# Loading one operand three tiles ahead instead of four in a batched 64x64 matmul

## The chip, the cores and the metric

The kernel runs on one core of a Trainium2 chip, the other cores idle. In the profiles PE is TensorE (PEld its weight loads), DVE is VectorE, ACT is ScalarE, POOL is GpSimd and SP is SyncE; SP, ACT and POOL also issue the DMA transfers, and a load lands when its bytes are all in place. The metric is the device time of one execution in microseconds (us), as the median of several runs. All comparisons below use runs that were marked fast; a ratio is the mean time of one kernel's fast runs over the mean time of the other kernel's fast runs of the same rounds, so it is not quite the ratio of the two medians that stand beside it.

## The reference

```python
a = np.random.randn(1024, 64, 64).astype(np.float32)
b = np.random.randn(1024, 64, 64).astype(np.float32)
out = np.matmul(a, b).astype(np.float32)
```

Each of the three tensors is 16.78 MB. There is little arithmetic for that many bytes, so the kernel is mostly a matter of moving data.

## The kernel before

The batch is cut into 16 tiles of 64 matrices. Tile `t` of b is 1 MB and lives in one of `B_AHEAD` buffers. a comes in 8 steps of 128 matrices; three quarters of a step are loaded from POOL's queue and cast to bf16 on the way (`a_sb`), the last quarter is loaded raw from SP's queue (`a_raw`). Only the first step is loaded raw as a whole, from SP and ACT. Even tiles of b are issued on SP, odd ones on ACT. Stores are issued on POOL.

```python
    A_AHEAD = 3
    B_AHEAD = 4
    HOLD = 2
    # ...
    b_pool = ctx.enter_context(tc.tile_pool(name="b_pool", bufs=B_AHEAD))
    o_pool = ctx.enter_context(tc.tile_pool(name="o_pool", bufs=8))
    # ...
    def load_b(t):
        b_sb = b_pool.tile([128, 16, 128], fp32, name="b_sb")
        queue = nc.scalar if t % 2 else nc.sync
        queue.dma_start(out=b_sb[:], in_=b_v[t])
        b_tiles[t] = b_sb
    # ...
        for t in range(n_t):
            s, half = t // 2, t % 2
            if t + 1 < n_t:
                spread(t + 1)            # VectorE: a into block-diagonal form
                cast(t + 1)              # VectorE: b to bf16, frees the b buffer
            if t + B_AHEAD < n_t:
                load_b(t + B_AHEAD)      # waits for the cast of tile t
            if half == 0 and 0 < s < n_s - 1 - A_AHEAD:
                load_a(s + 1 + A_AHEAD)
            # ...
            multiply(t)                  # TensorE, then copies out of PSUM on ACT and VectorE
            if t == 0:
                regroup(1)
                load_a(A_AHEAD)
                load_a(A_AHEAD + 1)
            # ... regroup (VectorE), transpose (TensorE, ACT) of later steps of a
            if t >= HOLD - 1:
                store(t - HOLD + 1)      # POOL's queue
```

The last tile but one is stored in two pieces and the last in four; all others in one piece of 1 MB.

Of the kernel before, what the change touches and what calls it, by code (L numbers as in the profile page):

```python
# [13 lines left out]
def kernel(  # L14
# [18 lines left out]

    n_t, n_s = B // 64, B // 128
    A_AHEAD = 3
    B_AHEAD = 4
    N_BD = 2
    HOLD = 2

# [5 lines left out]
    a_pool = ctx.enter_context(tc.tile_pool(name="a_pool", bufs=A_AHEAD))  # L45
    b_pool = ctx.enter_context(tc.tile_pool(name="b_pool", bufs=B_AHEAD))
    work = ctx.enter_context(tc.tile_pool(name="work", bufs=2))
# [16 lines left out]
    def load_a(s):  # L64

        a_sb = a_pool.tile([128, 3, 16, 64], bf16, name="a_sb")
        for h in range(3):
            nc.gpsimd.dma_start(  # L68
                out=a_sb[:, h, :, :].rearrange("p v k -> p (v k)"), in_=a_v[s, h]
            )  # L70
        a_raw = a_pool.tile([128, 16, 64], fp32, name="a_raw")
        nc.sync.dma_start(out=a_raw[:].rearrange("p v k -> p (v k)"), in_=a_v[s, 3])  # L72
        a_tiles[s] = a_sb, a_raw

    def load_first_a():

        raw = [
            o_pool.tile([128, 8, 2, 2, 64], fp32, name="o_sb")[:].rearrange(
                "p gh j wl n -> p (gh j wl n)"
            )  # L80
            for _ in range(2)
        ]
        parts = [raw[h % 2][:, 1024 * (h // 2) : 1024 * (h // 2) + 1024] for h in range(4)]
        for h in range(4):
            (nc.scalar if h % 2 else nc.sync).dma_start(out=parts[h], in_=a_v[0, h])  # L85
        a_tiles[0] = parts
# [7 lines that stand above are left out]
    def regroup(s):  # L94
        a_sb = a_tiles.pop(s)
        a_bf = work.tile([128, 16, 4, 64], bf16, name="a_bf")
        if s == 0:
            for h in range(4):
                copy = nc.scalar.copy if h % 2 else nc.vector.tensor_copy
                copy(a_bf[:, :, h, :], a_sb[h].rearrange("p (v k) -> p v k", v=16))  # L100
        else:
            cast_sb, raw = a_sb
            nc.vector.tensor_copy(  # L103
                a_bf[:, :, 0:3, :], cast_sb[:].rearrange("p h v k -> p v h k")
            )
            nc.vector.tensor_copy(a_bf[:, :, 3, :], raw[:])  # L106
        abf_tiles[s] = a_bf
        at_tiles[s] = work.tile([128, 2, 32, 2, 4, 4], fp32, name="at_sb")

    def transpose(s, j):  # L110
        a_cols = abf_tiles[s][:].rearrange("p v h k -> p v (h k)").bitcast(fp32)
        for wl in range(2):
            at_ps = t_psum.tile([128, 4, 128], fp32, name="at_ps")
            for vo in range(4):
                nc.tensor.transpose(  # L115
                    at_ps[:, vo, :], a_cols[:, 4 * vo + 2 * j + wl, :], identity[:]
                )
            nc.scalar.copy(  # L118
                at_tiles[s][:, j, :, wl, :, :],
                at_ps[:].rearrange("p vo (g mp) -> p g mp vo", mp=4),  # L120
            )

    def spread(t):
        half = slice(16 * (t % 2), 16 * (t % 2) + 16)
        bd = bd_tiles[t % N_BD]
        for h in range(4):
            rows = slice(32 * h, 32 * h + 32)
            nc.vector.tensor_copy(  # L128
                bd[rows, :, :, :, h, :].rearrange("p j g wl mo -> p j (g wl) mo"),
                at_tiles[t // 2][rows, :, half, :, :, :].rearrange(  # L130
                    "p j g wl mp vo -> p j (g wl) (mp vo)"
                ),
            )

    def cast(t):
        b_bf = work.tile([128, 16, 128], bf16, name="b_bf")
        b_sb = b_tiles.pop(t)
        if t < n_t - 1:
            (nc.vector.tensor_copy if t else nc.scalar.copy)(b_bf[:], b_sb[:])  # L139
        else:  # L140
            for gq in range(4):
                rows = slice(4 * gq, 4 * gq + 4)
                if gq % 2:
                    nc.vector.tensor_copy(b_bf[:, rows, :], b_sb[:, rows, :])
                else:
                    nc.scalar.copy(b_bf[:, rows, :], b_sb[:, rows, :])  # L146
        bbf_tiles[t] = b_bf

    def store(t):
        for piece in held.pop(t):  # L150
            piece()
# [53 lines left out]
    with tc.manual_schedule():  # L205
        load_first_a()

        nc.vector.memset(warm[:, 0:1], 0.0)
        nc.scalar.copy(warm[:, 1:2], warm[:, 0:1])  # L209
        load_b(0)  # L210
        load_b(1)
        nc.vector.memset(bd_tiles[0][:], 0.0)  # L212
        make_identity(nc, identity)
        nc.gpsimd.memset(bd_tiles[1][:, 0], 0.0)
        load_a(1)
        load_b(2)
        nc.gpsimd.memset(bd_tiles[1][:, 1], 0.0)  # L217
        load_a(2)
        regroup(0)
        transpose(0, 0)  # L220
        transpose(0, 1)
        load_b(3)
        spread(0)
        cast(0)
        for t in range(n_t):
            s, half = t // 2, t % 2
            if t + 1 < n_t:
                spread(t + 1)
                cast(t + 1)
            if t + B_AHEAD < n_t:  # L230
                load_b(t + B_AHEAD)
            if half == 0 and 0 < s < n_s - 1 - A_AHEAD:
                load_a(s + 1 + A_AHEAD)
            if half == 0 and 0 < s < n_s - 1:
                transpose(s + 1, 1)
            multiply(t)
# [4 lines that stand above are left out]
                transpose(1, 0)  # L241
                transpose(1, 1)
            elif t == 1:
                regroup(2)
            elif half == 0 and s + 2 < n_s:
                regroup(s + 2)
            if half == 1 and s + 2 < n_s:
                transpose(s + 2, 0)
            if t >= HOLD - 1:
                store(t - HOLD + 1)  # L250
        for t in range(n_t - HOLD + 1, n_t):
            store(t)
# [30 lines left out]
```

## Time and profile before

| what | value | where it is read |
|---|---|---|
| median time | 135.42 us (135.24 to 135.50) | 3 runs |
| span of the profiled run | 133.8 us | head of the page |
| read and written | 33.55 MB and 16.78 MB | the HBM line |
| VectorE busy, ACT busy | 71%, 66% | part 1 |
| last b tile issued, landed | 94.05 us, 110.45 us | timeline of ACT, 16.4 us to landing |
| last product copied out of PSUM | 121.37 us | timeline of ACT, 118.34 + 3.03 |
| last store issued | about 122.4 us | timeline of POOL |

Busy shares of 71% and 66% suggest that no engine is the limit, and over the whole span none is. The row of the DMA engines tells more, because it is full from the second slice to the last but one. The prediction shows these lines. A detail for reading them is that a load with a cast counts its written bytes, half of what it reads, so slices with many of them show about 310 GB/s although the engines are no less busy.

### The profile page before, as it was taken

Reading aid. Unit: us, or ns where it says so; the run is one execution under the profiler, and the core shown is the slowest. Engines: PE = TensorE matmul, PEld = TensorE weight load, DVE = VectorE, ACT = ScalarE, POOL = GpSimd, SP = SyncE. Lnnn points to the kernel's source line nnn. Section 1 sums busy time; section 2 is a strip of 40 time slices with the busy share of each in tenths; the row PEclk is TensorE's granted clock in tenths of the full one; section 3 lists DMA queues with packets and bytes.
Section 4 is the critical chain, followed back from the end, with each engine's and each line's share of the span. In section 5 each row is a group of like instructions: output and inputs, shape, how many; then the busy total and the mean of one; then the engine's idle time right before and its main releaser. Section 6 shows DMA issues by size and latency. Waiting matters only on the chain.

```text
span 133.8 us, 2832 instructions
## 1 busy us (share of the span) xinstructions
PE 65.7 (49%) x1152; PEld 62.7 (47%) x1152; DVE 94.6 (71%) x120; ACT 87.7 (66%) x161; POOL 38.5 (29%) x49
## 2 busy tenths in 40 slices
PE   0007307970077463749919744991876376640000
PEld 0007207970077353649909744991866266630000
DVE  5930499108997059999999999899959989992000
ACT  3225424998038996758998985899793987992000
POOL 8991000420091080334124042003301220637000
PEclk9999999999559999555996896589677775797555
DMA  3999999999999999999999999999999999999991
GB/s 75 376 331 311 306 315 311 307 301 309 306 307 382 366 312 309 388 397 397 317 304 352 399 392 377 314 307 364 398 385 391 392 401 398 404 388 353 338 334 42
DMA packets 17485, 45.01 MB, mean 336 GB/s; under 512 B 1088, under 2 KB 1088, under 8 KB 17472
## 3 DMA queue, kind: packets, MB, share of 16 engines
q0 software_dynamic: 7440, 22.28, 54.8%
q1 hardware_dynamic: 5520, 13.11, 27.0%
q10 hardware_dynamic: 4512, 9.44, 18.6%
q8 instruction: 9, 0.15, 0.4%
q14 instruction: 4, 0.03, 0.1%
HBM read 33.55 MB, written 16.78 MB: 376 GB/s over the span
## 4 chain that ended last, share of the span: by engine, by line
DMA 35%; SPq 27%; DVE 15%; issue 6%; ACT 3%; POOL 3%; PE 3%; POOLq 1%; DVEq 0%; ACTq 0%
SPq L72 22%; DMA a_raw<-in_a_dram 18%; DMA b_sb<-in_b_dram 17%; DVE at_bd L128 8%; DVE b_bf L139 5%; SPq L91 3%; POOL out_dram L161 3%; PE o_ps L184 3%; ACT o_sb L172 2%; DVE o_sb L172 1%; SPq L85 1%; ACT b_bf L146 1%; DVE a_bf L106 1%; DVE a_bf L103 1%; POOLq L278 1%
## 5 line engine op out<-in xcount | busy, mean ns | idle before, releaser
L172 ACT COPY o_sb<-o_ps 64x512 f32<-64x512 f32 x106 | 61.6, 581 | 14.3 <-PE o_ps L184 13.0
L184 PEld LDWEIGHTS <-at_bd 128*128 128x128 bf16 x1024 | 41.6, 111 | 34.9 <-DVE b_bf L139 22.4
L184 PE MATMUL o_ps<-b_bf,at_bd 128*128 128x64 bf16 x960 | 41.9, 215 | 31.1 <-DVE b_bf L139 20.9
L128 DVE COPY at_bd<-at_sb 32x1024 f32<-32x1024 f32 x64 | 46.0, 719 | 13.4 <-ACT at_sb L118 11.6
L161 POOL DMA_DIRECT2D out_dram<-o_sb x20 | 20.6, 1031 | 58.1 <-ACT o_sb L172 21.4
L115 PE MATMUL at_ps<-identity,a_bf 128*128 128x128 f32 x128 | 23.4, 360 | 20.6 <-ACT a_bf L100 11.0
L115 PEld LDWEIGHTS at_ps<-identity,a_bf 128*128 128x128 f32 x128 | 21.6, 196 | 20.8 <-issue 19.3
L118 ACT COPY at_sb<-at_ps 128x512 f32<-128x512 f32 x32 | 16.9, 596 | 8.2 <-PE at_ps L115 8.0
L68 POOL DMA_DIRECT2D a_sb<-in_a_dram x21 | 13.9, 673 | 25.9 <-DVE a_bf L103 19.9
L139 DVE CAST b_bf<-b_sb 128x2048 bf16<-128x2048 f32 x14 | 17.4, 1245 | 2.9 <-DMA b_sb<-in_b_dram 2.6
L172 DVE COPY o_sb<-o_ps 64x512 f32<-64x512 f32 x14 | 9.7, 690 | 0.6 <-ACT o_sb L172 0.3
L106 DVE CAST a_bf<-a_raw 128x1024 bf16<-128x1024 f32 x7 | 5.5, 792 | 5.7 <-DMA a_raw<-in_a_dram 5.7
L103 DVE COPY a_bf<-a_sb 128x3072 bf16<-128x3072 bf16 x7 | 7.0, 1006 | 0.0
L100 ACT CAST a_bf<-o_sb 128x1024 bf16<-128x1024 f32 x2 | 2.1, 1044 | 5.0 <-DMA o_sb<-in_a_dram 5.0
L139 ACT CAST b_bf<-b_sb 128x2048 bf16<-128x2048 f32 x1 | 1.9, 1898 | 3.8 <-DMA b_sb<-in_b_dram 3.8
L100 DVE CAST a_bf<-o_sb 128x1024 bf16<-128x1024 f32 x2 | 2.8, 1380 | 1.9 <-DMA o_sb<-in_a_dram 1.9
L212 DVE MEMSET at_bd<- 128x4096 f32 x1 | 3.5, 3472 | 0.8 <-issue 0.8
L172 DVE COPY o_sb<-at_ps 64x256 f32<-64x256 f32 x8 | 3.4, 422 | 0.3 <-PE at_ps L184 0.2
L172 ACT COPY o_sb<-at_ps 64x256 f32<-64x256 f32 x8 | 2.9, 367 | 0.1
L209 ACT ACT_TABLE_LOAD x1 | 1.3, 1283 | 2.3 <-issue 2.3
L184 PE MATMUL at_ps<-b_bf,at_bd 128*128 128x64 bf16 x64 | 2.0, 193 | 1.2 <-DVE at_bd L128 1.2
L217 POOL MEMSET at_bd<- 128x2048 f32 x1 | 1.8, 1849 | 0.0
(12 smaller groups left out, 5.5 us busy)
## 6 DMA issues: line engine op xcount, KB each, us to landing
out_dram<-o_sb POOLq DMA_DIRECT2D x14, 1024.0 KB, 23.6
a_sb<-in_a_dram POOLq DMA_DIRECT2D x21, 256.0 KB, 17.4
a_raw<-in_a_dram SPq DMA_DIRECT2D x7, 512.0 KB, 24.2
o_sb<-in_a_dram ACTq DMA_DIRECT2D x2, 512.0 KB, 7.0
o_sb<-in_a_dram SPq DMA_DIRECT2D x2, 512.0 KB, 5.9
out_dram<-o_sb POOLq DMA_DIRECT2D x2, 512.0 KB, 11.4
out_dram<-o_sb POOLq DMA_DIRECT2D x4, 256.0 KB, 10.1
b_sb<-in_b_dram SPq DMA_DIRECT2D x8, 0.5 KB, 22.2
```

Source lines behind the costliest of these rows:

```text
L68: nc.gpsimd.dma_start(out=a_sb[:, h, :, :].rearrange("p v k -> p (v k)"), in_=a_v[s, h])
L72: nc.sync.dma_start(out=a_raw[:].rearrange("p v k -> p (v k)"), in_=a_v[s, 3])
L100: copy(a_bf[:, :, h, :], a_sb[h].rearrange("p (v k) -> p v k", v=16))
L103: nc.vector.tensor_copy(a_bf[:, :, 0:3, :], cast_sb[:].rearrange("p h v k -> p v h k"))
L106: nc.vector.tensor_copy(a_bf[:, :, 3, :], raw[:])
L115: nc.tensor.transpose(at_ps[:, vo, :], a_cols[:, 4 * vo + 2 * j + wl, :], identity[:])
L118: nc.scalar.copy(at_tiles[s][:, j, :, wl, :, :], at_ps[:].rearrange("p vo (g mp) -> p g mp vo", mp=4),)
L128: nc.vector.tensor_copy(bd[rows, :, :, :, h, :].rearrange("p j g wl mo -> p j (g wl) mo"), at_tiles[t // 2][rows, :, half, :, :, :].rearrange(
L139: (nc.vector.tensor_copy if t else nc.scalar.copy)(b_bf[:], b_sb[:])
L161: nc.gpsimd.dma_start(out=o_v[t, :, lo : lo + n, :], in_=o_sb[:, lo : lo + n].rearrange("p gh j wl n -> p (gh j wl n)"),)
L172: copies[2 * par + wl](dst, src)
L184: nc.tensor.matmul(o_ps[:, gl, g % 2, j, :], at_bd[:, j, g, :, u], b_bf[:, g, 64 * u : 64 * u + 64], start=(u == 0), stop=(u == 1),)
```

## The change

The intent is to need one b buffer less (8 KB of each partition), on the guess that three tiles ahead are enough.

```diff
-    B_AHEAD = 4
+    B_AHEAD = 3
@@
         transpose(0, 0)
         transpose(0, 1)
-        load_b(3)
         spread(0)
         cast(0)
```

## The prediction

> **What bounds the kernel now.** I read the page's slices first, to see whether anything is full all the time.
>
> ```profile
> DVE  5930499108997059999999999899959989992000
> ACT  3225424998038996758998985899793987992000
> DMA  3999999999999999999999999999999999999991
> GB/s 75 376 331 311 306 315 311 307 301 309 306 307 382 366 312 309 388 397 397 317 304 352 399 392 377 314 307 364 398 385 391 392 401 398 404 388 353 338 334 42
> HBM read 33.55 MB, written 16.78 MB: 376 GB/s over the span
> ```
>
> The row to look at is DMA: after the first of the 40 slices (3.3 us each) it never drops below 9 until the last one. The slices with 301 to 317 GB/s are not slack: there the queue from POOL loads a as fp32 and writes it as bf16, and the rate counts the written bytes. The kernel must move 33.55 + 16.78 = 50.33 MB; from about 2.5 us to 131 us that is 50.33 MB / 128.5 us = 392 GB/s. The window table gives the same rate where nothing is cast, and shows the end:
>
> ```profile
> 100.00:110.50 10.50, 5.83 (x128) 5.46 (x128) 9.87 (x13) 7.69 (x14) 2.26 (x2) 0.75 1.03 395
> 110.50:120.00 9.50, 5.66 (x128) 5.38 (x128) 8.76 (x15) 8.59 (x18) 3.03 (x3) 0.74 1.02 397
> 120.00:123.10 3.10, 0.00 (x0) 0.00 (x0) 1.06 (x3) 1.34 (x4) 2.85 (x4) 0.86 1.02 358
> 123.10:126.00 2.90, 0.00 (x0) 0.00 (x0) 0.00 (x0) 0.00 (x0) 0.00 (x0) 0.50 1.02 346
> 126.00:129.00 3.00, 0.00 (x0) 0.00 (x0) 0.00 (x0) 0.00 (x0) 0.00 (x0) 0.50 1.00 341
> 129.00:131.00 2.00, 0.00 (x0) 0.00 (x0) 0.00 (x0) 0.00 (x0) 0.00 (x0) 0.50 0.75 275
> 131.00:132.00 1.00, 0.00 (x0) 0.00 (x0) 0.00 (x0) 0.00 (x0) 0.00 (x0) 0.50 0.10 41
> ```
>
> The last two columns are DMA share and GB/s. All engines are done at about 123 us; for 8 us more the DMA engines only drain stores. So the end is set by bytes, not by the last product. In the middle VectorE is nearly full too (9.70 of 10 us in 50 to 60, 9.67 and 9.74 in the next two), which paces a b tile at about 5.9 us (the casts start at 51.70, 57.51, 63.36, 68.91, 75.01 us). Because VectorE runs ahead of the stores, a backlog of stores builds up, and that backlog is the 8 us at the end.
>
> Next I read who waits for a load:
>
> ```profile
> DVE a_bf L106 <- DMA a_raw<-in_a_dram: 5.7, 1, 5.7
> DVE b_bf L139 <- DMA b_sb<-in_b_dram: 2.6, 4, 1.5
> SPq L91 <- DVE b_bf L139: 2.2, 3, 1.3
> ```
>
> Waits for b cost VectorE 2.6 us in all, in four pieces. So four buffers are just enough: some b tiles arrive within a fraction of a microsecond of their use.
>
> **What the Trainium skill says.** "DMA: Bandwidth & Descriptors", section "Issuing engines are not separate DMA queues", says that copies issued from SP, ACT and POOL run on the same 16 engines and interleave. The trace agrees: b alone on ACT's queue takes 15.6 to 17.4 us from issue to landing for 1 MB, far longer than 1 MB at 392 GB/s (2.7 us). The same page, "Queues, rings and completion order", says each engine takes turns between queue rows packet by packet. I use that for the share that a queue gets: when one queue has nothing, the others get its turns. "HBM Reference", "Specifications (TRN2)", puts a core streaming alone at about 425 GB/s, bounded by its 16 engines; this trace sustains 392 to 397, so the page's figure leaves at most some 8% that this kernel does not reach before or after.
>
> **The change part by part.** No instruction of compute is added or removed, and no byte: 16 loads of b remain, of 1 MB each. One b buffer disappears, so the load of tile t+4 waits for the cast of t+1 instead of the cast of t, and it stands one turn of the loop later in its queue. The order of the built program shows three shifts.
>
> First, b tile 3 leaves the prologue. It was issued on ACT at 14.77 us; now it stands after the cast of tile 0 there (19.07 + 1.90 us), so at about 21 us, 6 us later. It landed at 14.77 + 16.8 = 31.6 us and was cast at 40.16, so 8.6 us of slack cover that. By 14.77 us, without b tile 3, these had been asked for: a's first 2.1 MB, three tiles of b (3.1 MB), two raw quarters of a (1 MB), nine cast quarters (4.7 MB read): 11 MB, or 28 us of work at 392 GB/s. DMA does not run dry.
>
> Second, on SP the third and fourth raw quarters of a now stand ahead of b tile 4.
>
> ```profile
> 23.19 0.71 SPq L91 DMA_DIRECT2D b_sb<-in_b_dram  x1
> 23.95 13.28 SPq L72 DMA_DIRECT2D a_raw<-in_a_dram  x2
> 48.22 0.69 DVE L106 CAST a_bf<-a_raw 128x1024 bf16<-128x1024 f32 x1 [5.71 <-DMA a_raw<-in_a_dram]
> ```
>
> Before, the raw quarters queued behind 1 MB of b, and VectorE stood 5.71 us for the first. With b behind them I expect the quarter some 8 us earlier (1 MB at the 115 GB/s that SP's queue got here, 1.5 MB between b landings 13 us apart) and most of that wait gone. B tile 4 then lands about 5 us later, at 51 instead of 46.1, against a cast at 51.70. So some 3 to 5 us come back there, part of them lost again to b.
>
> Third, the steady part. Issues on SP and their landings:
>
> ```profile
> 53.02 0.71 SPq L91 DMA_DIRECT2D b_sb<-in_b_dram  x1
> 64.74 0.71 SPq L91 DMA_DIRECT2D b_sb<-in_b_dram  x1
> 70.22 0.70 ACTq L91 DMA_DIRECT2D b_sb<-in_b_dram  x1
> 82.13 0.70 ACTq L91 DMA_DIRECT2D b_sb<-in_b_dram  x1
> 94.05 0.69 ACTq L91 DMA_DIRECT2D b_sb<-in_b_dram  x1
> ```
>
> The two on SP (tiles 8 and 10) took 20.8 and 22.1 us to land, so 73.8 and 86.9; their casts began at 75.01 and 86.92. Those on ACT (11, 13, 15) took 16.4, 16.1 and 16.4, so 86.6, 98.2 and 110.4, for uses at 92.73, 105.86 and 111.75. Now each is issued 5 to 6 us later. If latency stayed, three buffers would carry one tile per (19.4 + 1.3) / 3 = 6.9 us instead of 5.9, and from tile 5 on the slip would reach about 11 us. But part of that latency is waiting behind the queue's own previous load: landings on ACT follow each other by 11.6 to 12.2 us, so a load that finds its queue empty needs some 12 us plus a little, not 16.4, and the queue that is empty meanwhile leaves its turns to the other. With 12 to 15 us the period is (13.5 + 1.3) / 3 = 4.9 to 5.4 us, below the 5.9 of VectorE. Tile by tile I get: 9 on time, 11 on time, 13 about 2 us late, 15 at 114 to 117 us instead of 110.4. So the last tile slips by 3 to 6 us.
>
> What does that slip cost? The last store of 256 KB is issued at 122.4 us and takes 10.0 us to land, because 8 us of stores stand before it. Alone I estimate 3 us for it (it is 0.7 us of bytes at 392 GB/s and some 2 us of fixed time; an estimate). So 7 us of slip are free: the bytes that were drained after 123 us have been drained earlier, in the turns that b did not take. Sum: bytes unchanged 0; start 0; slip of 3 to 6 us against 7 us of cover 0; a few tenths for the smaller overlap of stores and tail, either way: 135.4 + 0.2 = 135.6 us.
>
> **The rivals.** One: the loop of three buffers is too short for the landing times, and tiles stall as if latency stayed at 19.4 us. For it speaks that tiles 10, 12 and 14 already arrive just at their use (waits of 0.3, 1.5 and 0.3 us). Against it, latency shrinks when less is outstanding. The slip would be 11 us, 7 covered, so some 4 us visible: about 139.5 us. Two: fewer b loads in the way bring a's raw quarters forward, VectorE starts its full stretch 4 us earlier, and stores begin earlier. For it, the 5.71 us wait. Against it, DMA is full at that time whoever gets the turns, so an earlier compute only lengthens the drain: 135 us. Three: the drain at the end ran at 341 to 358 GB/s instead of 395; if later loads shift part of it into the mixed stretch, 3 MB move at 395 instead of 345: 8.7 - 7.6 = 1.1 us gained, 134.3 us. Against it, 110 to 120 us was almost all stores and ran at 397, so stores alone are not what is slow.
>
> **Range and chances.** The first story and rivals two and three all lie between 134.3 and 136; the stall lies at 139.5, and a partial stall between. I give the stall beyond 138.1 us (2% of 135.42) one chance in seven, and the bytes allow no gain beyond 2%: 132.7 us would need the whole transfer at about 400 GB/s. So 135.6 us, 8 in 10 between 134.3 and 138.0; faster 0.03, same 0.83, slower 0.14.
>
> **What would show it.** In the changed profile the DMA row should still read 9 from the second slice to the last but one; the wait of VectorE for the raw quarter should fall from 5.7 us to under 2; waits of VectorE for b should rise from 2.6 us to 5 to 10; landing on ACT should fall from 16.4 us to 12 to 15; the last b should land at 114 to 117 us, and the drain after the last compute should shrink from 8 us to 2 to 5. I am wrong if the DMA row shows holes, or if the last compute ends after 130 us: then rival one holds and the drain is used up.

## The result, and the profile after

The changed kernel took 134.81 us (134.71 to 134.94, 4 runs) against 135.45 us of the kernel before. The ratio is 0.9956 with a 95% interval of 0.9939 to 0.9973. By the 2% rule this is the same, but the interval leaves out 1, so a small gain of 0.6 us is real.

These are the rows of the slices and the line of bytes on the page of the changed kernel.

```profile
DMA  3999999999999999999999999999999999999991
GB/s 80 374 333 310 308 311 279 284 304 327 327 312 400 317 322 329 399 387 396 313 284 367 407 389 359 305 307 390 396 394 388 394 394 391 403 402 402 383 339 39
HBM read 33.55 MB, written 16.78 MB: 379 GB/s over the span
```

The DMA row is as full as before, and the bytes are the same. The rates differ near the end: slices 36 to 38, counted from 1, read 402, 402 and 383 GB/s, where the kernel before has 388, 353 and 338 in slices 36 to 38 (the slices are 3.3 us long in both).

The table of windows of the changed kernel, over the same windows as in the prediction, shows it in time. Columns are the window, its length, busy us of PE, PEld, VectorE, ACT and POOL, the granted clock, the DMA share and GB/s.

```profile
100.00:110.50 10.50, 6.47 (x134) 6.02 (x133) 10.17 (x13) 8.34 (x16) 2.26 (x2) 0.83 1.03 392
110.50:120.00 9.50, 5.85 (x118) 5.45 (x115) 6.71 (x11) 5.84 (x11) 1.35 (x1) 0.67 1.03 400
120.00:123.10 3.10, 1.09 (x26) 0.97 (x23) 2.99 (x8) 3.00 (x7) 1.19 (x2) 0.90 1.02 398
123.10:126.00 2.90, 0.00 (x0) 0.00 (x0) 0.07 (x1) 2.25 (x7) 2.02 (x4) 0.66 1.02 388
126.00:129.00 3.00, 0.00 (x0) 0.00 (x0) 0.00 (x0) 0.00 (x0) 1.16 (x2) 0.50 1.00 347
129.00:131.00 2.00, 0.00 (x0) 0.00 (x0) 0.00 (x0) 0.00 (x0) 0.00 (x0) 0.50 0.41 156
131.00:132.00 1.00, 0.00 (x0) 0.00 (x0) 0.00 (x0) 0.00 (x0) 0.00 (x0) 0.50 0.00 0
```

Multiplying rate by length gives the bytes. From 120 us on, the kernel before moved 3.1 x 358 + 2.9 x 346 + 3 x 341 + 2 x 275 + 41 = 3730 KB and the changed kernel 3.1 x 398 + 2.9 x 388 + 3 x 347 + 2 x 156 = 3710 KB. So at 120 us the two had the same amount left, and all that happened before has cancelled out. The gain lies behind that point. From 120 to 126 us the changed kernel moved 2359 KB where the kernel before moved 2113 KB. Those 246 KB are 0.7 us at 345 GB/s, which is the gain within its error. In both kernels the rate falls from about 400 to about 345 GB/s near the end. In the changed kernel it falls some 6 us later.

Next come the waits of the changed kernel for loads (engine and line, what was waited for, total us, times, longest), the last of them from the list of SP's queue.

```profile
DVE b_bf L139 <- DMA b_sb<-in_b_dram: 8.7, 5, 3.5
ACT b_bf L146 <- DMA b_sb<-in_b_dram: 3.5, 1, 3.5
SPq L91 <- DVE b_bf L139: 8.1, 4, 3.3
```

VectorE's wait for the raw quarter of a (5.7 us before) is not in the list any more. In its place VectorE waits 8.7 us for b instead of 2.6, ACT waits 3.5 us for the last tile, and SP holds its b loads 8.1 us for a buffer instead of 2.2. The compute engines are worse served, and the time is a little shorter.

Five lines of the timelines of the changed kernel (start, length, what) show the three shifts.

```profile
10.52 13.76 SPq L72 DMA_DIRECT2D a_raw<-in_a_dram  x3
24.74 0.71 SPq L91 DMA_DIRECT2D b_sb<-in_b_dram  x1
41.82 0.68 DVE L106 CAST a_bf<-a_raw 128x1024 bf16<-128x1024 f32 x1
49.60 1.36 DVE L139 CAST b_bf<-b_sb 128x2048 bf16<-128x2048 f32 x1 [3.47 <-DMA b_sb<-in_b_dram]
101.70 0.69 ACTq L91 DMA_DIRECT2D b_sb<-in_b_dram  x1
```

The raw quarters now stand ahead of b tile 4 on SP, and the third is cast at 41.82 us instead of 48.22. Tile 4 in turn lands at 49.5 us (24.74 + 24.8) and VectorE stands 3.47 us for it, so the compute engines keep only part of what they won. The last b tile is issued at 101.70 us instead of 94.05. It takes 14.7 us instead of 16.4, so it lands at 116.4 instead of 110.45, 6 us later. The last copies out of PSUM end 4.1 us later:

```profile
122.41 3.03 ACT L172 COPY o_sb<-at_ps 64x256 f32<-64x256 f32 x8
```

That is 125.44 us against 121.37.

### The profile page after: what moved, and what is told of

Read it like the earlier page. It is cut to its first block, busy times and chain, and to the rows that moved or that the text cites. A ratio compares the mean times of both kernels' runs of the same rounds, so it can differ in the third digit from the quotient of the medians.

```text
span 132.9 us, 2839 instructions
## 1 busy us (share of the span) xinstructions
PE 65.2 (49%) x1152; PEld 61.7 (46%) x1152; DVE 95.0 (71%) x120; ACT 88.0 (66%) x161; POOL 37.2 (28%) x49
## 4 chain that ended last, share of the span: by engine, by line
DMA 43%; DVE 22%; issue 11%; ACT 10%; PE 6%; POOL 3%; SPq 1%; POOLq 1%; DVEq 0%
DMA b_sb<-in_b_dram 43%; DVE at_bd L128 11%; ACT o_sb L172 6%; DVE b_bf L139 4%; DVE o_sb L172 4%; POOL out_dram L161 3%; PE o_ps L184 3%; PE at_ps L115 3%; ACT at_sb L118 2%; ACT b_bf L139 1%; DVE a_bf L103 1%; SPq L85 1%; DVE a_bf L106 1%; POOLq L277 1%; SPq L91 1%
## 5 line engine op out<-in xcount | busy, mean ns | idle before, releaser
L184 PEld LDWEIGHTS <-at_bd 128*128 128x128 bf16 x1024 | 42.5, 113 | 40.0 <-DVE b_bf L139 26.2
L128 DVE COPY at_bd<-at_sb 32x1024 f32<-32x1024 f32 x64 | 47.1, 736 | 14.4 <-ACT at_sb L118 11.8
L161 POOL DMA_DIRECT2D out_dram<-o_sb x20 | 20.1, 1005 | 62.7 <-ACT o_sb L172 24.3
L115 PE MATMUL at_ps<-identity,a_bf 128*128 128x128 f32 x128 | 21.6, 340 | 19.2 <-ACT a_bf L100 11.0
L115 PEld LDWEIGHTS at_ps<-identity,a_bf 128*128 128x128 f32 x128 | 19.6, 182 | 19.3 <-issue 19.3
L118 ACT COPY at_sb<-at_ps 128x512 f32<-128x512 f32 x32 | 17.5, 590 | 11.1 <-PE at_ps L115 7.8
L68 POOL DMA_DIRECT2D a_sb<-in_a_dram x21 | 13.0, 634 | 26.7 <-DVE a_bf L103 19.4
L106 DVE CAST a_bf<-a_raw 128x1024 bf16<-128x1024 f32 x7 | 4.8, 684 | 0.0
L184 PE MATMUL at_ps<-b_bf,at_bd 128*128 128x64 bf16 x64 | 3.3, 233 | 1.2 <-DVE at_bd L128 1.2
L146 ACT CAST b_bf<-b_sb 128x512 bf16<-128x512 f32 x2 | 1.1, 615 | 3.5 <-DMA b_sb<-in_b_dram 3.5
## 6 DMA issues: line engine op xcount, KB each, us to landing
b_sb<-in_b_dram SPq DMA_DIRECT2D x8, 0.5 KB, 18.9
```

What stands on the lines that cost most here:

```text
L68: nc.gpsimd.dma_start(out=a_sb[:, h, :, :].rearrange("p v k -> p (v k)"), in_=a_v[s, h])
L106: nc.vector.tensor_copy(a_bf[:, :, 3, :], raw[:])
L115: nc.tensor.transpose(at_ps[:, vo, :], a_cols[:, 4 * vo + 2 * j + wl, :], identity[:])
L118: nc.scalar.copy(at_tiles[s][:, j, :, wl, :, :], at_ps[:].rearrange("p vo (g mp) -> p g mp vo", mp=4),)
L128: nc.vector.tensor_copy(bd[rows, :, :, :, h, :].rearrange("p j g wl mo -> p j (g wl) mo"), at_tiles[t // 2][rows, :, half, :, :, :].rearrange(
L161: nc.gpsimd.dma_start(out=o_v[t, :, lo : lo + n, :], in_=o_sb[:, lo : lo + n].rearrange("p gh j wl n -> p (gh j wl n)"),)
```

## The experiments

Theory A, formed after the result: the DMA engines are full from start to end, so the order of transfers does not matter except for the rate at the end. The drain of stores slows down some time after the last load, and loads that end later shorten the slow part. Rival B: the gain comes from the early part, where VectorE no longer stands 5.7 us for a. Rival C: it comes from having fewer loads in flight, that is from the missing buffer.

### The new order with the old number of buffers

```diff
 # the changed kernel (B_AHEAD = 3)
-    b_pool = ctx.enter_context(tc.tile_pool(name="b_pool", bufs=B_AHEAD))
+    b_pool = ctx.enter_context(tc.tile_pool(name="b_pool", bufs=4))
```

> The changed kernel's order of loads, but with four b buffers, so that no load of b waits for the buffer that the change took away. If the gain of 0.6 us comes from where the loads stand in their queues, this gives 134.8 us as the changed kernel does. If it comes from the wait for the buffer (fewer loads in flight), this gives 135.4 us as the kernel before. VectorE's wait for the raw quarter of a should be gone (under 1 us) in both cases, since a stands ahead of b tile 4.

Measured: 134.84 us against 135.28, ratio 0.9971 (0.9957 to 0.9985). As expected in both cases, VectorE's wait for the raw quarter is gone. The interval overlaps that of the changed kernel. Most of the gain comes without taking the buffer away (0.29% of 0.44% by the ratios), so rival C is not needed for it. Whether the missing buffer adds the rest, these intervals can't tell.

### Only the early part

```diff
 # the kernel before
-            if t + B_AHEAD < n_t:
+            if t and t + B_AHEAD < n_t:
                 load_b(t + B_AHEAD)
@@
                 load_a(A_AHEAD)
                 load_a(A_AHEAD + 1)
+                load_b(B_AHEAD)
```

> The kernel before with one thing alone: the third and fourth raw quarters of a stand ahead of b tile 4 on SP. Rival (the early part makes the gain, because VectorE no longer stands 5.7 us for the raw quarter): 134.8 us or less. Main theory (DMA is full, the end alone counts): 135.4 us within 0.3, the wait of 5.7 us gone, products finished up to 3 us earlier than 121 us, and a longer drain at the slow rate of 340 to 350 GB/s, so if anything 0.2 to 0.4 us slower.

Measured: 135.39 us against 135.28, ratio 1.0008 (0.9996 to 1.002). The wait of 5.7 us for a is gone, as meant, but it came back as a wait for b: 8.0 us instead of 2.6, 5.4 of them in one piece, so that the cast of b tile 4 starts at 51.27 us instead of 51.70. ACT's last copies end at 121.5 us, as in the kernel before and not earlier as I had thought possible; those of VectorE end at 122.7 instead of 121.1. Rival B falls in this form: putting a first and taking the wait for it away gives nothing. What less idle time of VectorE would be worth, the run does not show, because the wait was moved and not removed. The changed kernel casts tile 4 2.1 us earlier than the kernel before (49.60 us), but the traces show that lead gone by tile 8 (75.66 against 75.01 us).

### Only the last two loads later

```diff
 # the kernel before
-            if t + B_AHEAD < n_t:
+            if t + B_AHEAD < n_t - 2:
                 load_b(t + B_AHEAD)
+            if n_t - 2 <= t + 3 < n_t:
+                load_b(t + 3)
```

> The kernel before, only the last two loads of b stand one turn later. Main theory: the last products end some 3 to 5 us later, the stretch of slow drain (340 to 350 GB/s) shrinks by about as much, and the time falls by 0.3 to 0.7 us to 134.8 to 135.1. Rival (early part or fewer loads in flight): 135.4 us unchanged.

Measured: 134.98 us against 135.28, ratio 0.9975 (0.9961 to 0.9990). The last b landed at 114.0 us (99.79 + 14.2) and the products ended at 123.0. These are windows of the kernel before, then of this run; the last column is GB/s.

```profile
120.00:122.00 2.00, 0.00 (x0) 0.00 (x0) 1.06 (x3) 1.34 (x4) 1.75 (x3) 1.00 1.03 363
122.00:124.00 2.00, 0.00 (x0) 0.00 (x0) 0.00 (x0) 0.00 (x0) 1.09 (x2) 0.56 0.99 348
```

```profile
120.00:122.00 2.00, 0.71 (x14) 0.55 (x11) 1.93 (x5) 1.93 (x6) 0.96 (x2) 0.81 1.02 387
122.00:124.00 2.00, 0.00 (x0) 0.00 (x0) 0.52 (x2) 1.00 (x3) 1.89 (x3) 1.00 1.03 375
```

The two loads alone, with the order of everything before them untouched, give somewhat over half of the change's gain by the ratios (0.25% of 0.44%; the intervals overlap), and it appears where the theory puts it: the fast rate lasts longer. This supports A.

### The last two loads put back

```diff
 # the changed kernel, with bufs=4
-            if t + B_AHEAD < n_t:
+            if t + B_AHEAD < n_t - 2:
                 load_b(t + B_AHEAD)
+            if n_t - 2 <= t + 4 < n_t:
+                load_b(t + 4)
```

> The changed kernel's order with four buffers, but the last two loads of b stand one turn earlier, as in the kernel before. Main theory: the gain goes, 135.2 to 135.5 us. Rival: the gain of the early part stays, 134.8 us.

Measured: 135.00 us against 135.28, ratio 0.9987 (0.9969 to 1.0006). This lies between the two expectations and settles nothing by itself. The trace says why: the turns of the loop had already slipped, so the last b was issued at 96.67 us and landed at 114.6, not at 110.45. The edit did not put back what it was to put back.

### One step further: two tiles ahead

```diff
 # the changed kernel
-    B_AHEAD = 3
+    B_AHEAD = 2
@@
         load_a(1)
-        load_b(2)
```

> The change carried one step further: b two tiles ahead, two buffers. Main theory (a later end of the products is free until the drain is used up, then it costs in full): the last product end moves from 125.4 us to 131 or later, holes appear in the DMA row near the end, and the time goes over 137 us (slower by over 2%). If loads adapted without limit (latency shrinks as fewer are in flight), it stays at 134.8 or falls further.

Measured: 144.79 us in the median of three runs (a fourth, at 146.72, was slow and is left out) against 135.53, ratio 1.0654 (1.0613 to 1.0696). The last b landed at 128.4 us and the products ended at 137.3. The page's DMA row and two windows of this run:

```profile
DMA  3999999999999999999999999999899999984493
130.00:132.00 2.00, 2.00 (x42) 2.00 (x40) 1.06 (x3) 1.94 (x5) 0.00 (x0) 0.50 0.15 49
132.00:134.00 2.00, 0.58 (x11) 0.42 (x8) 1.92 (x6) 1.97 (x4) 0.77 (x1) 0.50 0.27 96
```

All stores that could be drained had been drained by 130 us, and the DMA engines then stood and waited for the last products. This is the edge that the changed kernel stays clear of. From 126 to 140 us the DMA shares add up to 9.2 us of 14, so 4.8 of the 9.2 us by which the span grew (143.0 against 133.8) are idle DMA. The rest stands in the rates before. These are the same windows of the kernel before, then of this run:

```profile
90.00:126.00 36.00, 17.73 (x365) 16.72 (x360) 28.01 (x40) 26.59 (x51) 10.72 (x11) 0.76 1.03 384
```

```profile
90.00:126.00 36.00, 21.43 (x408) 20.74 (x409) 30.19 (x38) 25.21 (x48) 7.14 (x6) 0.74 1.02 341
```

The DMA share is full in both, but this run moved 43 GB/s less, 1.5 MB in these 36 us, or about 4 us at 392 GB/s. In the stretch from 104 to 118 us mostly one queue of b at a time had packets moving, and these packets of 2 KB took 113 to 118 ns on average, where those of the kernel before took 85 to 89 in the same stretch. So a full DMA row does not by itself mean the full rate.

### One step the other way: five tiles ahead

```diff
 # the kernel before
-    B_AHEAD = 4
+    B_AHEAD = 5
@@
         load_b(3)
+        load_b(4)
```

> b five tiles ahead, five buffers: the change in the other direction. Main theory: the last b lands no later than in the kernel before, products end at or before 121 us, drain as slow: 135.4 to 135.8 us, so same as before within 0.4%. Rival (more loads in flight help because tiles wait less for b): under 135.0 us.

Measured: 135.81 us against 135.53, ratio 1.0026 (1.0013 to 1.0039), inside the range of theory A. More lookahead is slightly worse. The expectation that products end no later than 121 us was a miss; they ended at 123.5 on ACT and 124.7 on VectorE. That miss is useful, because here the end of the products and the end of the loads part ways:

```profile
118.00:120.00 2.00, 0.83 (x17) 0.75 (x16) 1.94 (x4) 1.91 (x5) 1.14 (x1) 0.50 1.06 379
120.00:122.00 2.00, 2.00 (x42) 2.00 (x40) 0.87 (x3) 1.94 (x5) 0.75 (x1) 0.50 0.98 346
```

The rate is down to 346 GB/s from 120 us on, with TensorE and ACT fully busy. So it is not the end of the products that slows the drain.

### What slows the drain: small pieces?

```diff
 # the kernel before
-        if last:
-            held[t] = [lambda q=q: put(2 * q, 2) for q in range(4)]
-        else:
-            whole = t < n_t - 2
-            held[t] = [lambda q=q: put(q, 8 if whole else 4) for q in ([0] if whole else [0, 4])]
+        held[t] = [lambda: put(0, 8)]
```

> The kernel before, but the last two tiles are stored in one piece each instead of two and four. Tells what makes the drain slow. If the small pieces do, packets stay at the fast rate (395 to 400 GB/s) to the end and the time falls to 134.4 to 134.9 us. If it is the end of compute or only stores being left, the drain is as slow as before (340 to 350 GB/s from about 121 us) and the time is 135.4 us, or up to 0.5 us more because the last store starts later.

Measured: 135.29 us against 135.53, ratio 0.9984 (0.9971 to 0.9997). From 122 to 130 us the rates were 342, 358, 320 and 338 GB/s, as slow as before. The small pieces are not the cause.

### What slows the drain: idle engines?

```diff
 # the kernel before, after the last store
+        idle = work.tile([128, 16, 128], bf16, name="b_bf")
+        for _ in range(4):
+            nc.scalar.copy(idle[:], bd_tiles[0][:, 0].rearrange("p g wl h mo -> p (g wl h mo)"))
```

> The kernel before with four copies on ACT added after the last product, from 121.4 to about 129 us, results unused. If the drain is slow because the engines are idle, it stays at 395 to 400 GB/s until 129 us and the time falls to 134.5 to 135.0 us. If it is slow because of the small store pieces or the lack of loads, nothing changes: 340 to 350 GB/s and 135.4 us.

Measured: 135.62 us against 135.53, ratio 1.0005 (0.9990 to 1.0020). ACT was busy from 121.54 to 129.23 us, and the rates from 122 to 130 us were 352, 336, 344 and 334 GB/s. An idle ACT is not the cause.

### What slows the drain: no loads beside it?

```diff
 # the kernel before, after multiply(t)
+            if t >= n_t - 2:
+                extra = work.tile([128, 16, 128], bf16, name="b_bf")
+                nc.sync.dma_start(
+                    out=extra[:].rearrange("p g n -> p (g n)").bitcast(fp32), in_=a_v[0, t - n_t + 2]
+                )
```

> The kernel before with two loads of a added (0.5 MB each, results unused), issued when the products of tile 14 and later are done, so that loads go on until about 120 us instead of 110. They add 1.05 MB, that is 2.7 us at 392 GB/s. In all runs so far the drain turned slow about 8 us after the last load had landed. If the end of the loads is what starts it, the slow part moves to about 128 us and the time grows by only 1.2 to 2.0 us, to 136.6 to 137.4. If the time or the stores' own place starts it, the slow part stays where it is and the time grows by the full 2.7 us, to 138.1 us.

Measured: 138.54 us against 135.50, ratio 1.0222 (1.0199 to 1.0245), somewhat more than the full 2.7 us. The edit did not do what I meant: the second load waited for the first, so they ran one after the other, issued at 116.2 and 125.7 us. By the packet records, the first moved its bytes only from 120 to 125 us. The rate fell to 371 GB/s from 118 to 120 us, before these bytes moved, and lower still while they began to; then it came back:

```profile
120.00:122.00 2.00, 0.93 (x18) 0.77 (x15) 1.92 (x6) 1.55 (x5) 1.43 (x2) 0.50 1.02 301
124.00:126.00 2.00, 0.00 (x0) 0.00 (x0) 0.00 (x0) 0.00 (x0) 0.00 (x0) 0.50 1.04 418
126.00:128.00 2.00, 0.00 (x0) 0.00 (x0) 0.00 (x0) 0.00 (x0) 0.00 (x0) 0.50 1.02 387
```

The kernel before has 346 and 342 GB/s in the last two of these windows, and this run is down to 322 again from 128 to 130 us. So a load beside the stores does not keep the rate up while it moves, but the fast rate returns behind it, for some 4 us and not for 8. That speaks for the loads as what matters, and against a fixed delay of 8 us.

### Loads that end later, meant to leave the products alone

```diff
 # the kernel before
                 load_b(t + B_AHEAD)
+                if t + B_AHEAD == n_t - 1:
+                    for h in range(2):
+                        extra = consts.tile([128, 1024], fp32, name=f"extra{h}")
+                        nc.scalar.dma_start(out=extra[:], in_=a_v[0, h])
```

> The added loads of the run before last waited for each other and did not do what I meant. Here the kernel before gets two loads of a (0.5 MB each, into tiles of their own, unused) right behind the last load of b on ACT's queue, so that loads go on without a gap from 110 to about 116 to 119 us while the products stay where they were. 1.05 MB more is 2.7 us at 392 GB/s. If the end of the loads is what starts the slow drain about 8 us later, it starts at 124 us or later instead of 118, and the time grows by 1.3 to 2.1 us, to 136.8 to 137.6. If something else starts it, the drain is slow from about 118 us as before and the time grows by 2.7 us or more, to 138.1 us or over.

Measured: 137.37 us against 135.44, ratio 1.0158 (1.0134 to 1.0183), 1.9 us more, inside the range of theory A. The loads ended at 115.3 us by the trace's packet records, and the rate was 391 GB/s from 122 to 124 us and 360 from 124 to 126, so the slow part came later, as it should if the end of the loads starts it. It isn't clean, though. These lines are from ACT's timeline of this run:

```profile
94.85 6.80 ACTq L235 DMA_DIRECT2D extra<-in_a_dram  x2
101.75 3.55 ACT L172 COPY o_sb<-o_ps 64x512 f32<-64x512 f32 x6 [7.47 <-issue]
```

Issuing the two extra loads held ACT for 6.80 us and delayed its copies by 7.47, and the products ended at 125.5 us instead of 121.4. So the stores were late too. Read with the run five tiles ahead, where the products were late and the slow part was not, it points to the loads, but it does not prove it.

### Two store queues, and a try at beating both kernels

```diff
 # the kernel before, and the same in the changed kernel
-            nc.gpsimd.dma_start(
+            queue = nc.sync if t >= n_t - 4 and t % 2 else nc.gpsimd
+            queue.dma_start(
                 out=o_v[t, :, lo : lo + n, :],
```

> The kernel before, with the stores of tiles 13 and 15 on SP's queue instead of POOL's. If a single queue of stores alone is what makes the drain slow, two queues keep it at 395 to 400 GB/s and the time falls to 134.4 to 134.9 us. If stores without loads are slow whatever their queue, 340 to 350 GB/s stays and the time is 135.4 us.

> The changed kernel with the same two store tiles on SP's queue: a try at a version that beats both. If two queues mend the drain, 134.2 to 134.6 us; if not, 134.8 us as the changed kernel.

Measured: in the kernel before 134.56 us against 135.50, ratio 0.9928 (0.9910 to 0.9947); in the changed kernel 134.55 us against the same, ratio 0.9924 (0.9908 to 0.9941). Windows of the first of the two:

```profile
122.00:124.00 2.00, 0.00 (x0) 0.00 (x0) 1.21 (x3) 0.35 (x1) 0.00 (x0) 0.50 1.04 365
128.00:130.00 2.00, 0.00 (x0) 0.00 (x0) 0.00 (x0) 0.00 (x0) 0.00 (x0) 0.50 1.01 340
```

The drain still slows down, to 365 and at last 340 GB/s, so one queue alone is not the whole cause either; but it slows less at first, and 0.9 us is gained. With two store queues the change adds nothing more. The two versions are the fastest I have, but their intervals overlap that of the changed kernel (0.9956 in its own rounds). The edit changed more than the queue: SP's stores stand in the trace as packets of 1,024 B, those of POOL as packets of 4,096 B.

### What the runs say together

| run | last b landed, us | products ended, us | median, us | ratio to before |
|---|---|---|---|---|
| before | 110.45 | 121.4 | 135.42 | 1 |
| a first | 110.3 | 121.5 | 135.39 | 1.0008 |
| tail late | 114.0 | 123.0 | 134.98 | 0.9975 |
| tail early | 114.6 | 123.6 | 135.00 | 0.9987 |
| order of three, four buffers | 115.1 | 124.1 | 134.84 | 0.9971 |
| changed kernel | 116.4 | 125.4 | 134.81 | 0.9956 |
| two ahead | 128.4 | 137.3 | 144.79 | 1.0654 |

(A landing is the issue in ACT's timeline plus its time to landing; the end of the products is the end of the last copies on ACT. VectorE's last copies end earlier or at most 0.3 us later, except in "a first", where they end at 122.7. The time before was 135.28 to 135.53 in the rounds of the experiments, so the ratios compare better than the medians.) Down to the changed kernel, later loads go with a slightly shorter time; much later ones cost.

In the traces of the runs that store from one queue and keep it full, the average store packet of 4 KB first took over 172 ns, instead of about 165, some 7 to 9 us after the last load packet (the run with the two loads that waited for each other is left out, since its loads began anew). In the kernel before that was at 118 us, with 12.3 of 16.8 MB stored; five tiles ahead it was at 118 us too, though the products ended later; in the changed kernel it was at 124 us, with 14.8 MB stored. So neither the end of the products nor the place of the stores in the output sets it. Two tiles ahead, where the stores had run dry before, the packets took over 180 ns within 1 us of the last load, so the 7 to 9 us are no constant. What happens in the hardware at that moment stays open. Small pieces and an idle ACT are ruled out, an added load brings the fast rate back only for a while, and a second queue only softens the fall.

## Why the prediction was right or wrong

The predicted class and range held: 134.81 us lies in 134.3 to 138.0, and the change is within 2%. The point, 135.6 us, missed by 0.8 us, and its sign against the kernel before was wrong, 0.2 us slower instead of 0.6 us faster.

**The bound.** That bytes and not products set the end was right. The DMA row stayed full, and the products ended 4.1 us later while the time fell.

**The three shifts.** The wait for the raw quarter was to fall from 5.7 us to under 2, and it vanished. B tile 4 was to land at about 51 us and landed at 49.5. Waits of VectorE for b were to rise to 5 to 10 us and rose to 8.7. The last b was to land at 114 to 117 us and landed at 116.4. The drain after the last issue of a store was to shrink from 8 us to 2 to 5, and about 4 are left. The packet records agree with the turns between queues that the prediction counted on: from 104 to 105 us of the kernel before there are 48 packets on each of the three queues.

**The latency.** Here the landing time came out right by another way than the one given, so that part is luck. I expected landing on ACT to fall from a median of 16.4 us to 12 to 15, hence a period of 4.9 to 5.4 us (by the formula the lower end should read 4.4), below VectorE's 5.9, so that the loop of buffers would not set the pace. ACT's median stayed at 16.5 us (14.7 to 17.3); only the last tile's load came down to 14.7. SP's fell from 22.2 us to 18.9, probably because its b loads stood behind less of their own queue. Put into the same formula, the two medians give (17.7 + 1.3) / 3 = 6.3 us, and the casts of tiles 4 to 14 were in fact 6.2 us apart on average (49.60 to 111.93 us) instead of 5.9 (51.70 to 110.38). So the loop did set the pace, as rival one said, but by 0.3 us a tile and not by 1.0.

**The cover.** Slip of 3 to 6 us was to be free because the last store had waited about 7 us behind others. The products slipped by 4.1 us and it was free; with two tiles ahead they ended 16 us later and the span grew by 9.2 us. The estimate of 3 us for the last store alone holds: two tiles ahead, where little stood before them, the last pieces of 256 KB landed 3.1 us after their issue. Rival one's visible stall came one step later than the change.

**The step that failed** is the last term of the sum, "a few tenths for the smaller overlap of stores and tail, either way". It had a sign and a size. Rival three had both nearly right: "3 MB move at 395 instead of 345: 8.7 - 7.6 = 1.1 us gained, 134.3 us". I set it aside because "110 to 120 us was almost all stores and ran at 397, so stores alone are not what is slow". The observation was true and the conclusion did not follow: stores alone ran fast for some 8 us after the last load in both kernels and slowly after that, so ending the loads 6 us later does shorten the slow part. The runs put that term at 0.3 us for the last two loads alone and 0.6 us for the whole change. It is less than rival three's 1.1 us because only part of the 3 MB left the slow stretch: the changed kernel still moved 1.35 MB at 347 GB/s and less from 126 us on.

## What to carry to other kernels

When the DMA row is full from end to end, look first for where the last products still meet a backlog of stores: until that was used up, later products cost nothing here. See how long the last store takes to land (10.0 us here, for a 256 KB piece), subtract what it takes alone (3.1 us here), and take the rest as the slip that is free. Beyond it the time grows, as the step from three tiles to two shows; there the thinner stream of loads also ran at a lower rate with the DMA row still full. When two versions move the same bytes, compare the rates in the last tenth of the span before looking anywhere else.

## What the Trainium skill lacked or had wrong

- "DMA: Bandwidth & Descriptors", "Where 436 GB/s comes from", says that for transfers between HBM and SBUF the HBM side, about 358 GB/s, binds. The one core at work ran at 392 to 400 GB/s over windows of about ten microseconds here. The statement in "HBM Reference", "Specifications (TRN2)", of about 425 GB/s for a core alone fits better.
- No page has the slow end of a store drain: about 400 GB/s for some 8 us after the last load, then mostly 320 to 365 until the end, in every run that stored from one queue and kept it full. What causes it was not found.
- "DMA: Bandwidth & Descriptors", "Issuing engines are not separate DMA queues", says that starting transfers from several engines only saves issue time. Moving two of the last four store tiles from POOL's queue to SP's made the kernel 0.9 us faster (ratio 0.9928). The sentence may still hold: whether the second queue, the different way of issuing or the smaller packets (1,024 B instead of 4,096) did it was not told apart.
- The same section calls the issue time usually small beside the transfer itself. Behind a load of b (0.71 us to issue on an otherwise empty queue) the next issue on SP took up to 13.70 us in the kernel before, and two loads added behind one on ACT held ACT for 6.80 us, so that its copies started 7.47 us late.
